# Low-rank up-projections of a recurrence, cut into eight pieces, each followed by a dense projection

## The chip, the core and the metric

The kernel runs on one core of a Trainium2 chip. A core has a matrix engine (TensorE, PE in the profile; its weight loads are PEld), a vector engine (DVE), a scalar engine (ACT), GpSimd (POOL) and a sync engine (SP), which here issues every DMA. Each engine works through its own list of instructions in order and waits at an instruction until the semaphores that it names have come. The metric is the device time of one execution in microseconds, the median over runs.

## What is computed

One layer of a model with 1024 tokens and 1024 channels: a norm, one wide projection, an attention branch with three kinds of keys, a recurrent branch (RWKV-7), a gated merge, and a feed-forward block with a short convolution. All inputs are float32. What matters for the change, shortened:

```
h = _rms_norm(x, norm_mix);  u = h @ w_in
q, kc, vc, ks, vs, kw, vw, nsa_gl, rw, merge = _split(u, IN_SPLITS)
o_nsa = _nsa(q, kc, vc, ks, vs, kw, vw, nsa_gl, ...)        # attention
# recurrent branch, on z = rw
z = z + mu * (z_prev - z)                                   # token shift
r, k, v, wd, ad, gd = _split(z, RWKV_SPLITS)                # 512,512,512,64,64,128 columns
w = -softplus(-(w0 + tanh(wd) @ w_up)) - 0.5;  decay = exp(-exp(w))
a = sigmoid(a0 + ad @ a_up)
g = sigmoid(gd) @ g_up
kh = k * (1 + (a - 1) * k_a);  kk = normalised k * k_k per head
y = _wkv7_scan(r, decay, kh, v, -kk, kk * a)                # then norm, bonus, * g
y = gates[0] * (o_nsa @ proj_nsa) + gates[1] * (o_rwkv @ proj_rwkv);  x = x + y @ w_out
x = x + _conv_ffn(_rms_norm(x, norm_ffn), ffn_up, ffn_conv, ffn_down)
```

The products with `w_up`, `a_up` and `g_up` (64, 64 and 128 rows) are the low-rank up-projections.

## The kernel before

Activations lie transposed, channels on partitions and tokens along the free axis, in two halves of 512 tokens. A dense projection (`project`, line 229) makes 128 output columns: `wload` (line 214) loads a weight tile `wraw` of 512 KB, ACT copies it to a rounded `whi`, POOL makes the rest `wlo`, and `mm3` (line 224) then does 24 matmuls of 128 x 512 for each half of the tokens into a PSUM tile `psP`. A whole projection is thus 48 matmuls at line 226. Tiles tagged "P" take turns on two PSUM banks, so a third one waits until the first has been read out.

The program is written as one chain of attention work (`attention`, a generator) into which a list of **fillers** is woven: the attention yields weights, and each time they sum to one, one filler is emitted behind it with a priority 10000 lower. A scheduler then sets the order on each engine by these priorities and a timeline of its own. So PE does attention where that scheduler expects it to be ready, and fillers elsewhere. After the attention, the remaining fillers are emitted in a row.

The fillers are:

- `zproj(g)`, line 575: one of 14 projections for the recurrence. Each half is shifted by one token with ACT (line 582) and DVE (line 583) into a tile `zs` and stored to `z_d`. `zs` is a ring of three buffers (`NZS`), which all fillers share. Projection 12 is [wd, ad], 13 is gd, 0 to 3 are r, 4 to 7 k, 8 to 11 v.
- `loraproj`, line 809, a generator: for each half `h` it loads `zwa` and `zg` (projections 12 and 13), takes tanh, and then for each of four column blocks `j` does three float32 matmuls (line 825): decay, `a` and gate. Each has its own `psP` tile. ACT takes tanh of the first two into a `zs` tile (line 831) and copies the third (line 828); POOL scales (lines 835 and 838); four tiles are stored by DMA to `lw_d`, `km_d`, `al_d` and `gt_d`. In the trace a float32 matmul stands as two records. Before the change the generator yields once for each half, after its four blocks.
- `prelude(j, h)`, line 745, in three steps, eight of them: it reads back r, k and the four low-rank results of one block and half and makes the operands of the recurrence. Its second step starts with a matmul at line 781, its third does 32 small ones at line 798. It stores to `ar_d`, `rk_d`, `bk_d` and `ad_d`.
- `mproj(m, halves)`, line 592: 16 projections for the gates, the last eight of them for one half only here (24 matmuls); the other halves follow later.

The attention goes through four pairs of heads. The projection of the next pair's queries (`qproj`, line 424) also uses "P" banks: its result stays in the bank until a norm (`rms64`: ACT line 297, PE line 299, ACT lines 301 and 302, DVE line 303) has read it.

Weight column groups of `w_t` are numbered: 4 to 7 are the queries, 8 to 21 are `zproj` 0 to 13, 22 to 37 are `mproj` 0 to 15.

When the attention and the listed fillers are done, the recurrence starts. Its first load (`gmk`, then `AD` for a small triangular solve) waits for the PE matmul with which the last projection of the first part ends, since its tiles take over the memory of that part.

## Time and profile before

| what | value |
|---|---|
| time, median of 3 runs | 1833.86 us (1833.84 to 1838.98) |
| span of the profiled execution, first to last instruction | 1828.3 us |
| granted TensorE clock, mean | 0.984 |
| DVE busy | 1168.6 us (64%) |
| ACT busy | 856.7 us (47%) |
| POOL busy | 773.4 us (42%) |
| first and last low-rank matmul start | 159.5 and 267.4 us |

The profiled execution's own time outside the span is not given; the median lies 5.6 us above its span. Busy time of PE includes the time in which matmuls run at a lower clock, and the ends of matmuls are modelled, so that a busy PE is not always one at full speed. In a timeline a row gives start, length, engine, line, operation, tiles, and in brackets the idle time ahead of it and what ended it. In a table of windows a row gives the stretch, its length, busy time (and number of instructions) of PE, PEld, DVE, ACT and POOL, the granted clock, the DMA share and GB/s.

### The profile page before, as it was taken

The numbers are of one execution on the slowest core, as the hardware profiler recorded it, in microseconds if no ns is written. First come the engines' busy times: TensorE is split into PE (matmuls) and PEld (weight loads), VectorE is DVE, ScalarE is ACT, GpSimd is POOL, SyncE is SP. The second block draws the span as 40 slices with busy tenths as digits, with TensorE's granted clock in tenths as the row PEclk, the third lists the DMA queues.
The fourth block names the chain that finished last, engine by engine and source line by source line (L and its number), as shares of the span: only waits on it lengthen the run. The fifth ranks groups of instructions, "written<-read, shape, count | busy, mean of one in ns | idle before, by whom it ended". The sixth has DMA issues, their size and how long they took to land.

```text
span 1828.3 us, 30848 instructions
## 1 busy us (share of the span) xinstructions
PE 1764.1 (96%) x11890; PEld 1375.4 (75%) x11890; DVE 1168.6 (64%) x2005; ACT 856.7 (47%) x1574; POOL 773.4 (42%) x500
## 2 busy tenths in 40 slices
PE   8999999999999999999999979998999999999998
PEld 5885657776777778777777768886888888888886
DVE  6214656777776511984445364419998899886798
ACT  5234665657656632455555454333443343534330
POOL 5212133131333325211234545566455444667757
PEclk9998999999999999899999989999999999999999
DMA  5415143231334435445553465343332222433302
GB/s 179 127 53 172 42 156 104 68 121 58 119 131 136 132 125 187 153 150 171 168 180 116 159 207 166 115 144 127 127 117 97 87 81 89 163 140 127 127 12 104
DMA packets 133443, 230.19 MB, mean 126 GB/s; under 512 B 25008, under 2 KB 54064, under 8 KB 133040
## 3 DMA queue, kind: packets, MB, share of 16 engines
q1 hardware_dynamic: 133296, 228.21, 37.6%
q8 instruction: 94, 1.54, 0.3%
q14 instruction: 53, 0.43, 0.1%
HBM read 159.39 MB, written 63.96 MB: 122 GB/s over the span
## 4 chain that ended last, share of the span: by engine, by line
PE 40%; DVE 7%; issue 1%; ACT 1%; DMA 1%; POOL 1%; POOLq 0%; DVEq 0%; SPq 0%; ACTq 0%
PE psP L226 9%; PE psM L1389 5%; PE psA L1389 3%; PE psP L1389 3%; PE psA L226 3%; PE psB L1499 2%; PE psA L1499 1%; PE psM L1499 1%; PE psP L1499 1%; PE psB L226 1%; PE psP L1570 1%; DVE u L1265 1%; PE psA L1570 1%; PE psM L1570 1%; PE psB L1570 1%
## 5 line engine op out<-in xcount | busy, mean ns | idle before, releaser
L220 POOL TENSOR_TENSOR wlo<-wraw,whi 128x1024 fp32r<-128x1024 f32 (+1 forms) x106 | 231.1, 2185 | 409.1 <-ACT whi L219 151.2
L226 PE MATMUL psP<-hhi,whi 128*128 128x512 f32 x784 | 319.3, 408 | 15.1 <-ACT hhi L706 8.9
L226 PE MATMUL psP<-hlo,whi 128*128 128x512 f32 x784 | 316.1, 404 | 3.8 <-DVE hlo L707 2.4
L226 PE MATMUL psP<-hhi,wlo 128*128 128x512 f32 x784 | 208.5, 399 | 0.0
L226 PEld LDWEIGHTS psP<-hhi,whi 128*128 128x128 f32 x784 | 149.3, 191 | 51.3 <-ACT hhi L706 10.6
L226 PEld LDWEIGHTS psP<-hlo,whi 128*128 128x128 f32 x784 | 149.3, 191 | 38.9 <-DVE hlo L707 3.8
L226 PEld LDWEIGHTS psP<-hhi,wlo 128*128 128x128 f32 x784 | 146.1, 190 | 31.8 <-issue 0.5
L219 ACT ACTIVATE whi<-wraw 128x1024 fp32r<-128x1024 f32 (+1 forms) x106 | 101.8, 961 | 131.6 <-PE psP L226 76.8
L543 DVE TENSOR_TENSOR pl<-pf,ph 128x512 f16<-128x512 f32 (+3 forms) x208 | 123.6, 604 | 44.2 <-ACT pf L542 43.2
L541 ACT ACTIVATE ph<-psA 128x512 f16<-128x512 f32 (+3 forms) x208 | 99.3, 477 | 62.1 <-PE psA L536 43.8
L484 DVE TENSOR_REDUCE mp<-psM 128x1 f32<-128x512 f32 (+1 forms) x192 | 94.5, 514 | 45.4 <-PE psM L482 38.5
L542 ACT ACTIVATE pf<-psA 128x512 f32<-128x512 f32 (+3 forms) x208 | 99.9, 480 | 0.0
L1330 POOL TENSOR_TENSOR wlo<-wraw,whi 128x1024 fp32r<-128x1024 f32 (+1 forms) x34 | 73.5, 2163 | 54.8 <-PE psM L1389 20.3
L546 PEld LDWEIGHTS <-ph 128*128 128x128 f16 x592 | 55.8, 97 | 22.6 <-issue 12.3
L565 POOL TENSOR_TENSOR onat<-onat,ot 128x256 f32<-128x256 f32 x32 | 25.0, 783 | 111.8 <-DVE ot L564 88.8
L551 PEld LDWEIGHTS <-pl 128*128 128x128 f16 x592 | 55.4, 99 | 20.7 <-DVE pl L543 6.5
L1329 ACT ACTIVATE whi<-wraw 128x1024 fp32r<-128x1024 f32 (+1 forms) x34 | 30.8, 910 | 64.1 <-issue 29.7
L549 PEld LDWEIGHTS <-ph 128*128 128x128 f16 x592 | 56.1, 98 | 2.1 <-issue 2.0
L1273 DVE SCALAR_TENSOR_TENSOR th<-th,u 128x512 f32<-128x512 f32 x34 | 56.8, 1670 | 0.4
L1330 POOL TENSOR_TENSOR s34l<-s,s34h 128x1024 fp32r<-128x1024 f32 x12 | 30.0, 2498 | 61.5 <-ACT s34h L1329 61.5
L721 DVE SCALAR_TENSOR_TENSOR fu<-psP,par,fu 128x511 f32<-128x511 f32 (+1 forms) x40 | 29.9, 746 | 34.9 <-ACT cvl L719 34.3
L969 DVE STREAM_TRANSPOSE AT<-AD 128x1024 f32<-128x1024 f32 x2 | 4.4, 2187 | 68.0 <-DMA sg_d<-zs 68.0
(711 smaller groups left out, 4879.0 us busy)
## 6 DMA issues: line engine op xcount, KB each, us to landing
wraw<-f_up SPq DMA_DIRECT2D x64, 512.0 KB, 3.3
wraw<-w_t SPq DMA_DIRECT2D x46, 512.0 KB, 3.8
wraw<-f_dn SPq DMA_DIRECT2D x22, 512.0 KB, 3.9
th_d<-th SPq DMA_DIRECT2D x34, 256.0 KB, 2.1
sg_d<-zs SPq DMA_DIRECT2D x32, 256.0 KB, 2.0
wraw<-w_out SPq DMA_DIRECT2D x16, 512.0 KB, 3.4
z_d<-zs SPq DMA_DIRECT2D x28, 256.0 KB, 2.4
x<-xT SPq DMA_DIRECT2D x24, 256.0 KB, 5.6
```

What stands on the lines that cost most here:

```text
L219: A.activation(hi[:, :nk], raw, AF.Copy)
L220: G.tensor_sub(lo[:, :nk], raw, hi[:, :nk].bitcast(F32))
L226: T.matmul(ps, a[:, k], ks_(b, k), start=(n == 0), stop=(n == 3 * nk - 1))
L484: V.reduce_max(mp[:, x, br, t:t + 1], pm[:, 0:(b1 - b0) * 128], axis=AX.X)
L541: A.activation(ph[0:nkey, rg], pa[0:nkey, rg], AF.Exp, scale=0.125)
L542: A.activation(pf[0:nkey, rg], pa[0:nkey, rg], AF.Exp, scale=0.125)
L543: V.tensor_sub(pl[0:nkey, rg], pf[0:nkey, rg], ph[0:nkey, rg])
L1273: V.scalar_tensor_tensor(th, th, 0.5, ub, op0=ALU.mult, op1=ALU.mult)
L1330: G.tensor_sub(lo[:, ks], raw[:, ks], hi[:, ks].bitcast(F32))
L1389: T.matmul(bank, w[wi][:, o_ + k], xs_[k][xi], start=start and n == 0, stop=n == 11, skip_group_check=True)
L1499: T.matmul(pj, x[:, m], y, start=(n == 0), stop=(n == 5))
L1570: T.matmul(pj, w[x][:, 4 * kp + j], hs[kp][y], start=(n == 0), stop=(n == 5))
```

## The change

`loraproj` now yields after each column block, so it comes in eight pieces of three matmuls, and each piece is put into one filler with a dense projection behind it. The order of the dense projections changes with it: before, 12, 13, 0, half of the low-rank work, 4, the other half, 8, then the preludes with the other nine between their steps; now 12, 13, 0, then a piece each with 4, 1, 5, 2, 6, 3, 7 and 8, then the preludes with 9, 10, 11 and the gate projections between their steps. Since a piece and a projection are one filler, more is emitted for the same number of filler turns.

```
-                yield
+                    yield
...
         lo_ = loraproj()
-        fillers = [(zproj, 12), (zproj, 13), (zproj, 0), (step, lo_), (zproj, 4), (step, lo_), (step, lo_), (zproj, 8)]
-        rest = [(zproj, q_ + j_) for j_ in range(1, 4) for q_ in (0, 4, 8)] + mp_
+        def lproj(gi):
+            step(lo_)
+            zproj(gi)
+
+        fillers = [(zproj, 12), (zproj, 13), (zproj, 0)] + [(lproj, g_) for g_ in (4, 1, 5, 2, 6, 3, 7)] + [
+            (lproj, 8), (step, lo_)]
+        rest = [(zproj, g_) for g_ in (9, 10, 11)] + mp_
         for j_ in range(4):
             for h_ in range(2):
                 g_ = prelude(j_, h_)
                 fillers += [(step, g_), rest.pop(0), (step, g_), rest.pop(0), (step, g_)]
```

The number of instructions and their operands stay the same; the order moves. Three places matter. Lines up to 840 keep their numbers.

On PE at the start of the low-rank work before (line 825 is low-rank, 478 and 482 are attention scores):

```order
L825 MATMUL psP<-zwa,lora 128x512
L825 MATMUL psP<-zg,lora 128x512
L478 LDWEIGHTS qd
L478 MATMUL psM<-k1s_322,qd 128x512
L478 LDWEIGHTS qd
L478 MATMUL psM<-k1s_322,qd 128x256
L482 LDWEIGHTS identb
L482 MATMUL psM<-cb,identb 128x128
L825 MATMUL psP<-zwa,lora 128x512
```

The same place on PE now, where the last rows are the dense projection 4 (line 226):

```order
L825 MATMUL psP<-zwa,lora 128x512
L825 MATMUL psP<-zg,lora 128x512
L478 LDWEIGHTS qd
L478 MATMUL psM<-k1s_322,qd 128x512
L478 LDWEIGHTS qd
L478 MATMUL psM<-k1s_322,qd 128x256
L482 LDWEIGHTS identb
L482 MATMUL psM<-cb,identb 128x128
L226 MATMUL psP<-hhi_107,whi 128x512
L226 MATMUL psP<-hlo_115,whi 128x512
```

After three low-rank matmuls, 48 dense ones stand where nine more low-rank matmuls stood; all eight pieces look like this.

On PE at the norm of the third pair's queries (line 299 is the norm's matmul, 532 to 536 and 551 are attention) before:

```order
L532 MATMUL psA<-qd,k1w_326 128x512
L534 LDWEIGHTS k2w_327
L534 MATMUL psA<-q_2965,k2w_327 128x512
L536 LDWEIGHTS identb
L536 MATMUL psA<-cb,identb 128x128
L299 MATMUL psM<-nsq,cst_f 128x512
L532 LDWEIGHTS k1w_326
```

The end of the same norm on PE now, its second half (the rows just ahead of these are the end of the query projection itself, line 226, with the norm's first half two matmuls before its end, and eight short matmuls of line 490):

```order
L490 LDWEIGHTS qd
L490 MATMUL psM<-k1c_332,qd 128x64
L492 LDWEIGHTS identb
L492 MATMUL psM<-cb,identb 128x512
L299 MATMUL psM<-nsq,cst_f 128x512
L226 MATMUL psP<-hhi_107,whi 128x512
L226 MATMUL psP<-hlo_115,whi 128x512
```

Before, attention matmuls stood between the query projection and both halves of its norm; now the norm follows at once, and the next dense projection (number 9) follows the norm.

On PE at the last prelude (line 798 is its third step, 226 the gate projections, 570 the last step of the attention) before:

```order
L226 MATMUL psP<-hhi_91,wlo 128x512
L570 MATMUL psA<-cst_f,onat 128x128 x8
L226 MATMUL psP<-hhi_92,wlo 128x512
L798 MATMUL psP<-lw,BK 64x64 x16
L226 MATMUL psP<-hhi_107,whi 128x512
```

And now (line 551 is attention):

```order
L551 LDWEIGHTS pl
L551 MATMUL psB<-Vc,pl 128x65
L226 MATMUL psP<-hhi_113,wlo 128x512
L226 MATMUL psP<-hhi_114,wlo 128x512
L798 MATMUL psP<-lw,BK 64x64 x16
L226 MATMUL psP<-hhi_107,whi 128x512
```

Before, 240 dense matmuls stood between this step and the start of the recurrence, and 48 between the prelude's second step and this one; now there are 72 and 24. From the start of the recurrence on, PE's order is as before up to the seam where the recurrence ends and the feed-forward block begins; there some matmuls of lines 226 change places with each other.

## The prediction

> **What bounds the kernel now.** I read the page first, then windows over the stretch that the change reorders, then the timeline of PE, ACT and SP there.
>
> ```profile
> span 1828.3 us, 30848 instructions
> PE   8999999999999999999999979998999999999998
> PEclk9998999999999999899999989999999999999999
> ```
>
> PE is busy nearly everywhere, so time can only be won where PE idles or runs at a lower clock. Both are seen in the fourth slice (137 to 183 us), where the low-rank matmuls begin.
>
> ```profile
> 716.74 1.99 PE L226 MATMUL psP<-hhi,wlo 128*128 128x512 f32 x8
> ...
> 718.76 0.33 SPq L139 DMA_DIRECT2D gmk<-cst  x1
> 719.14 0.43 SPq L139 DMA_DIRECT2D AD<-ad_d  x1
> ...
> 723.94 2.26 DVE L969 STREAM_TRANSPOSE AT<-AD 128x1024 f32<-128x1024 f32 x1 [67.97 <-DMA sg_d<-zs]
> ```
>
> These rows fix the far end. The recurrence starts when the last projection of the first part ends (718.7 us), although DVE has by then been idle for most of 68 us: the start is tied to PE's matmul, not to the preludes. PE does the same matmuls between 159.5 us and this point before and now. So the change is worth what idle time and slow clock it takes from or adds to these 559 us; the rest shifts with it.
>
> ```profile
> 159.50:184.90 25.40, 22.50 (x71) 7.88 (x70) 11.66 (x22) 7.99 (x13) 9.32 (x12) 0.80 0.52 175
> 196.60:224.90 28.30, 24.84 (x328) 16.72 (x327) 24.51 (x60) 23.49 (x55) 3.08 (x2) 1.00 0.06 20
> 239.00:267.80 28.80, 25.93 (x204) 12.71 (x204) 18.10 (x35) 17.91 (x39) 10.88 (x13) 0.94 0.46 160
> 316.40:339.20 22.80, 21.57 (x276) 14.15 (x276) 21.22 (x53) 18.08 (x46) 3.45 (x3) 1.00 0.07 25
> 339.20:413.10 73.90, 73.90 (x639) 54.35 (x637) 52.05 (x111) 43.67 (x102) 21.79 (x16) 1.00 0.37 113
> 443.00:663.50 220.50, 217.48 (x1847) 162.04 (x1845) 136.26 (x278) 127.44 (x294) 75.25 (x52) 1.00 0.38 125
> 663.50:718.60 55.10, 55.09 (x241) 45.22 (x242) 0.00 (x0) 16.58 (x23) 19.98 (x9) 1.00 0.42 139
> ```
>
> The columns after the length are busy time of PE, PEld, DVE, ACT and POOL. The first and third rows are the two low-rank halves: PE idles 2.90 and 2.87 us and the clock is 0.80 and 0.94. The second and fourth are attention without dense matmuls after a query projection (3.46 and 1.23 us idle). Where dense projections are mixed in (fifth and sixth rows) PE idles 3.02 us in 294, at full clock.
>
> **What the low-rank block costs.**
>
> ```profile
> 159.49 1.12 PE L825 MATMUL psP<-zwa,lora 64*128 64x512 f32 x2
> ...
> 168.24 1.12 PE L825 MATMUL psP<-zwa,lora 64*128 64x512 f32 x2 [1.45 <-ACT zs L828]
> ...
> 171.36 2.07 PE L825 MATMUL psP<-zwa,lora 64*128 64x512 f32 x2
> ...
> 243.49 1.12 PE L825 MATMUL psP<-zg,lora 128*128 128x512 f32 x2 [1.70 <-ACT zs L831]
> ...
> 167.59 0.60 ACT L828 ACTIVATE zs<-psP 128x512 f32<-128x512 f32 x1 [4.56 <-DMA lw_d<-zs]
> ```
>
> Each block of three matmuls fills four `zs` tiles, and the ring has three: the gate's copy (line 828) waits until the decay's store has landed, 4.56 us in this row. ACT stands still, the PSUM bank stays full, and PE waits for the bank (1.45 us). The next matmul then takes 2.07 us where the same took 1.12.
>
> ```profile
> 166.75:170.17 3.42, 1.97 (x7) 0.77 (x7) 1.14 (x3) 1.97 (x3) 0.62 (x1) 1.00 0.63 228
> 170.17:180.41 10.24, 10.24 (x22) 3.49 (x21) 3.54 (x7) 2.57 (x4) 3.38 (x5) 0.50 0.56 196
> 241.85:245.26 3.41, 1.77 (x4) 0.59 (x4) 2.37 (x3) 2.46 (x7) 3.33 (x3) 1.00 0.00 0
> 245.26:248.67 3.41, 3.41 (x17) 1.40 (x16) 2.32 (x6) 1.77 (x3) 1.36 (x2) 0.50 0.73 226
> 412.50:415.90 3.40, 2.18 (x25) 1.61 (x25) 0.77 (x3) 0.45 (x1) 3.15 (x4) 1.00 0.22 78
> ```
>
> Here the clock falls to 0.50 for 10.24 and 3.41 us, each time after 3.4 us in which PE was busy 58% and 52%. After a 64% busy one (last row) it stays at 1.00. So the gaps of 1.45 and 1.70 us seem to have cost the clock as well: half of 10.24 is 5.12 us, half of 3.41 is 1.71.
>
> The Trainium skill, "TensorE: Matmul & The Clock Gate", section "HAM oscillation — how this bites in real kernels", gives as the abstract rule "no PE-idle gaps >~3.4µs". By it gaps of 1.45 and 1.70 us would be harmless, the slow clock would have another cause, and the sum below would lose its clock term; these rows speak against that, since both slow stretches begin right behind the two longest gaps. It is the first rival below.
>
> **The sum, part by part**, against the span of 1828.3 us:
>
> 1. *Idle in the two low-rank halves*: between 0 and -5.77 us. Now 48 dense matmuls, about 12 us by 0.25 us each (eight in the 1.99 us of the row at 716.74), follow each three low-rank ones, so the gate's bank has longer than the 4.56 us wait before it is needed. Every piece takes its three ACT, three POOL and four DMA instructions along. On SP they now stand ahead of weight loads, each issue 0.3 to 0.4 us; a store that waits for ACT holds the weight load behind it, but the next weights are loaded a projection ahead, 12 us. I take -5.2: some tenths stay in eight pieces.
> 2. *Clock*: -6.83 us if no window falls under the 58% any more; 0 if it is not due to gaps. I take -6.8.
> 3. *Attention without dense matmuls*: three such stretches before (the third, 413.1 to 443.0, follows the same pattern), two now, 358 and 394 matmuls where before 324, 274 and 346 stood. The 1.23 us of the fourth row go: -1.2, between 0 and -2.4 if the two others shrink too.
> 4. *The third query projection*: its norm now has nothing but eight short matmuls beside it.
>
> ```profile
> 333.83 0.59 PE L299 MATMUL psM<-nsq,cst_f 128*128 128x512 f32 x1
> ...
> 334.68 0.71 ACT L301 ACTIVATE nrs<-psM,epst 128x512 f32<-128x512 f32 x1
> ...
> 335.99 0.68 ACT L302 ACTIVATE nrs<-nrs 128x512 f32<-128x512 f32 x1
> ...
> 337.04 0.68 ACT L297 ACTIVATE nsq<-psP 128x512 f32<-128x512 f32 x1
> ```
>
>    In PE's order the second half's matmul (line 299) waits for ACT's square, which in ACT's order stands behind 301 and 302 of the first half: 0.71 + 0.68 + 0.68 = 2.1 us plus hand-overs behind PE's first norm matmul, against some 1.2 us of PE work between (two dense matmuls, eight short ones, one of 512). An idle time of about 1.5 us is near the ones that cost a slow window. I take +1.9: 1.5 and a quarter of 1.71. Bounds: 0, and 1.5 + 5.12 = 6.6 with three slow windows, as the first gap had. Queued behind the waiting matmul are projection 9 and the attention of the third pair.
> 5. *The end of the preludes*: the second and third step of the last one now have one half projection between them.
>
> ```profile
> 646.21 1.02 PE L781 MATMUL psP<-t,cst_f 128*128 128x512 f32 x2
> ...
> 651.42 0.68 DVE L785 TENSOR_TENSOR kk<-kk,t 128x512 f32<-128x512 f32 x1
> ...
> 654.00 0.69 DVE L789 TENSOR_TENSOR BK<-al,cum 128x512 f32<-128x512 f32 x1 [1.18 <-POOL al L788]
> ```
>
>    From 646.21 to 654.69 the chain took 8.5 us, beside attention's work on DVE and ACT. The cover is 24 x 0.25 = 6.0 us and 40 attention matmuls, some 2 us. I take +1.0 for the last preludes together, between 0 and 2.5 each for three.
> 6. *The first prelude beside projection 8*: its ACT steps now stand ahead of that projection's read-out (+0.5, between 0 and 1), and the seam behind the recurrence: 0, with one slow window (1.71) either way.
>
> Sum: -5.2 - 6.8 - 1.2 + 1.9 + 1.0 + 0.5 = -9.8 us. The span becomes 1818.5 us. The runs' median stands 5.6 us above the profiled span, so the forecast is 1833.9 - 9.8 = **1824.1 us**.
>
> **Rivals.**
>
> - *The slow clock stays.* The low-rank matmuls with 64 of 128 rows, or a phase of the clock's own, slow PE, not the gaps. Then term 2 goes and the gain is 3.0: 1830.9 us. For it: the gap at 168 us is followed by three slow windows, though PE was busy in them. Against: the first low-rank row, before any gap, is at full speed (1.12 us).
> - *The wait moves to the query projection.* Term 4 at its upper bound, 6.6 instead of 1.9: the gain is 5.1, 1828.8 us. For it: the order of the rows; against: the scheduler put a first norm matmul two ahead of the projection's end.
> - *The end turns into waits; slower.* The tail of 55 us, pure dense work with PE idle 0.01 us, takes in the last three preludes with half projections between their steps. If attention has run out there, each of three preludes waits 8.5 - 6.0 = 2.5 us, which is more than the idle time ahead of both slow stretches and so brings a slow 10.24 us (5.1 us): 3 x 7.6 = 22.8 in place of 1.0, which turns the gain of 9.8 into a loss of 12.0 us: 1845.9 us. It decides from the point where fewer than about 7.5 us of attention work (3 x 2.5) are left for the three gaps. Against: attention stands among the rows up to the last third step, and DVE and ACT have room.
> - *It doesn't do what it says*: the order shows that it does.
> - *More is won*: term 3 at its end, terms 4 to 6 at 0: -14.4, 1819.5 us; 1815 us if a slow window at the seam (1.7) and most of the 3.0 us idle in the sixth row of the first windows go too.
>
> **How the numbers follow.** Chances: forecast 0.60, clock stays 0.12, query projection 0.14, end of the preludes 0.07, more 0.07. The range from 1815 to 1832 us takes in all but the third rival and some of the forecast's spread. A measurement of this kernel can tell about 0.3%, 5.5 us, from no change (1828.4 to 1839.4 us). Faster by more: 0.58 of the forecast, 0.07 of the wins, half of the query case (0.07): 0.72. Within: 0.20. Slower: 0.08.
>
> **What would show it.** Right: the gate's copy (line 828) without a wait that PE feels; the clock at 1.00 from 159 us to the start of the recurrence; that start at about 709 us; from there on the same distances as before. Term 4 shows as idle time ahead of line 299 or the dense matmul behind it, with the clock after it; term 5 as idle time ahead of line 798. Wrong: a new slow window in the stretch, DVE or ACT behind the attention in the preludes, or a recurrence that starts earlier and ends no sooner.

## The result and the profile after

| | before | after |
|---|---|---|
| time, median | 1833.84 us | 1846.31 us |
| ratio after / before | | 1.0083, 95% interval 1.0062 to 1.0105 |
| span of the profiled execution | 1828.3 us | 1845.8 us (its time 1847.62 us) |
| issue of `gmk`, the start of the recurrence | 718.76 us | 735.37 us (forecast: about 709) |
| from there to the end of the span | 1109.5 us | 1110.4 us |

The change made the kernel 12.5 us slower by the medians (0.8%) where the forecast had it 10 us faster. The two profiled executions differ by more, 17.5 us in span: the span of the kernel before lies 5.5 us under its median time, that of the changed kernel 0.5 us. So some 5 us of the differences read from the two profiles are spread between executions. In the profiles all but 1 us of the loss lies ahead of the recurrence, as the prediction said that any difference would. The page of the changed kernel (span, PE's busy time, granted clock in 40 slices):

```profile
span 1845.8 us, 30848 instructions
PE 1769.7 (96%) x11876; PEld 1375.4 (75%) x11890; DVE 1186.2 (64%) x2005; ACT 857.9 (46%) x1574; POOL 774.6 (42%) x500
PEclk9999999999999999989999989999999999999999
```

The dent of the clock in the fourth slice is gone, yet the span is longer. Where the time went is seen in windows of the changed kernel (busy PE, PEld, DVE, ACT, POOL; clock):

```profile
159.50:187.80 28.30, 28.18 (x123) 19.87 (x123) 10.34 (x17) 6.93 (x10) 6.77 (x5) 1.00 0.35 112
187.80:224.90 37.10, 29.86 (x359) 20.12 (x360) 28.64 (x72) 24.51 (x57) 3.57 (x3) 0.91 0.05 16
224.90:251.00 26.10, 23.29 (x147) 15.03 (x146) 12.85 (x33) 16.19 (x31) 5.07 (x7) 0.93 0.27 81
655.90:729.70 73.80, 64.10 (x519) 48.09 (x517) 41.76 (x62) 42.02 (x97) 32.09 (x21) 0.95 0.49 157
```

The first row is what was hoped for: the first piece and its projection, PE idle 0.12 us, full clock. The second is attention behind the second query projection (7.2 us idle), the third the second piece and its projection (2.8 us), the fourth the last preludes (9.7 us idle). In the kernel before, the stretch from the first low-rank half's end to the same norm had 3.5 us idle in 40, at full clock:

```profile
184.90:224.90 40.00, 36.54 (x389) 26.05 (x385) 25.95 (x65) 26.80 (x60) 4.22 (x5) 1.00 0.13 41
```

What PE waits for in the second and third window, in the timeline of the changed kernel:

```profile
189.03 0.38 PE L478 MATMUL psM<-k1w,qd 128*128 128x512 f16 x1 [0.67 <-DVE mp L484]
...
192.67 0.39 PE L490 MATMUL psM<-k1c,qd 128*128 128x64 f16 x8 [0.67 <-DVE mp L484]
194.95 1.03 PE L504 MATMUL psM<-identh,Mt 128*128 128x128 f16 x8 [1.89 <-DVE Mt L500]
...
231.51 0.75 DVE L303 SCALAR_TENSOR_TENSOR qn<-psP,par,nrs 128x512 f32<-128x512 f32 x1 [1.94 <-ACT nrs L302]
232.32 1.12 PE L825 MATMUL psP<-zwa,lora 64*128 64x512 f32 x2 [2.12 <-DVE qn L303]
```

Scores (lines 478 to 490) that used to stand between low-rank matmuls now stand alone, and PE waits for DVE's maxima (0.67 us, four times) and for the matrix made of them (1.89 us). The second piece waits 2.12 us for a "P" bank that the query norm still reads. In the last window DVE is late, and with it the preludes:

```profile
688.11 4.53 DVE L543 TENSOR_TENSOR pl<-pf,ph 128x128 f16<-128x128 f32 x4
...
688.39 2.37 POOL L220 TENSOR_TENSOR wlo<-wraw,whi 128x1024 fp32r<-128x1024 f32 x1
...
691.10 0.20 PE L551 MATMUL psB<-Vw,pl 128*128 128x65 f16 x1 [2.22 <-DVE pl L543]
...
711.56 2.34 POOL L220 TENSOR_TENSOR wlo<-wraw,whi 128x1024 fp32r<-128x1024 f32 x1
711.63 2.81 DVE L789 TENSOR_TENSOR BK<-al,cum 128x512 f32<-128x512 f32 x1 [1.17 <-POOL al L788]
...
714.50 0.98 PE L798 MATMUL psP<-lw,BK 64*64 64x64 f32 x32 [3.26 <-DVE BK L789]
```

PE stands 3.26 us ahead of a prelude's third step (line 798), which waits for a DVE operation of 2.81 us; in the prediction's rows that operation took 0.69. The gap of 2.22 us is not a prelude's: it stands ahead of an attention matmul (line 551), which waits for four small DVE operations of the attention (4.53 us together) that ran partly beside a POOL subtraction.

The whole stretch up to the recurrence, split in both kernels where the first of the eight half projections begins (before, then after):

```profile
159.50:674.84 515.34, 499.31 (x4269) 352.54 (x4268) 328.44 (x715) 305.38 (x685) 150.10 (x124) 0.99 0.34 111
674.84:718.76 43.92, 43.92 (x193) 36.06 (x192) 0.00 (x0) 13.23 (x16) 19.30 (x8) 1.00 0.42 144
```

```profile
159.50:656.26 496.76, 477.80 (x3911) 336.44 (x3924) 304.34 (x654) 276.50 (x603) 136.95 (x111) 0.99 0.32 103
656.26:735.37 79.11, 69.41 (x536) 52.45 (x536) 41.40 (x61) 43.32 (x98) 34.14 (x22) 0.96 0.49 155
```

Up to that point PE idles 16.0 us before and 19.0 after; from there on 0 and 9.7.

The clock follows such gaps here too. These are the 3.41 us ahead of each of the four stretches in which the changed kernel's clock falls to 0.50 before the recurrence (for 6.8, 3.4, 3.4 and 3.4 us):

```profile
190.16:193.57 3.41, 1.48 (x16) 0.90 (x16) 2.26 (x7) 0.00 (x0) 0.28 (x1) 1.00 0.43 153
231.06:234.47 3.41, 1.97 (x7) 0.81 (x8) 2.03 (x5) 2.89 (x6) 1.31 (x2) 1.00 0.12 26
688.44:691.85 3.41, 1.18 (x24) 0.80 (x21) 3.41 (x3) 3.38 (x9) 3.18 (x2) 1.00 0.86 277
712.36:715.77 3.41, 0.98 (x32) 0.84 (x32) 3.30 (x7) 0.53 (x2) 1.98 (x2) 1.00 0.11 38
```

PE was busy 29 to 58% in each, as in the two cases of the prediction.

### The profile page after: what moved, and what is told of

Same layout as the page of the kernel before. It is cut to its first block, busy times and chain, and to the rows that moved or that the text cites. A ratio compares the mean times of both kernels' runs of the same rounds, so it can differ in the third digit from the quotient of the medians.

```text
span 1845.8 us, 30848 instructions
## 1 busy us (share of the span) xinstructions
PE 1769.7 (96%) x11876; PEld 1375.4 (75%) x11890; DVE 1186.2 (64%) x2005; ACT 857.9 (46%) x1574; POOL 774.6 (42%) x500
## 4 chain that ended last, share of the span: by engine, by line
PE 40%; DVE 7%; issue 1%; DMA 1%; POOL 1%; ACT 1%; SPq 0%; POOLq 0%; DVEq 0%; ACTq 0%
PE psP L226 9%; PE psM L1394 5%; PE psA L1394 3%; PE psP L1394 3%; PE psA L226 3%; PE psB L1504 2%; PE psA L1504 1%; PE psM L1504 1%; PE psP L1504 1%; PE psB L226 1%; PE psP L1575 1%; DVE u L1270 1%; PE psB L1575 1%; PE psM L1575 1%; PE psA L1575 1%
## 5 line engine op out<-in xcount | busy, mean ns | idle before, releaser
L226 PE MATMUL psP<-hhi,wlo 128*128 128x512 f32 x784 | 212.6, 401 | 0.0
L543 DVE TENSOR_TENSOR pl<-pf,ph 128x512 f16<-128x512 f32 (+3 forms) x208 | 133.8, 653 | 67.3 <-ACT pf L542 60.9
L565 POOL TENSOR_TENSOR onat<-onat,ot 128x256 f32<-128x256 f32 x32 | 28.8, 904 | 84.3 <-DVE ot L564 82.4
L1335 POOL TENSOR_TENSOR s12l<-s,s12h 128x1024 fp32r<-128x1024 f32 x12 | 31.4, 2620 | 34.4 <-PE psA L1394 21.3
```

What stands on the lines that cost most here:

```text
L226: T.matmul(ps, a[:, k], ks_(b, k), start=(n == 0), stop=(n == 3 * nk - 1))
L543: V.tensor_sub(pl[0:nkey, rg], pf[0:nkey, rg], ph[0:nkey, rg])
L1335: G.tensor_sub(lo[:, ks], raw[:, ks], hi[:, ks].bitcast(F32))
```

## The experiments

The loss has three suspects: the **cut** into pieces, the **order** of the dense projections that comes with it, and what either does to covers. In each run the start of the recurrence (issue of `gmk`, in one profiled execution) shows the part in question; the ratio is that of many executions to the kernel before in the same session. Executions of one kernel spread by some 5 us to either side, so a start alone is good to a few microseconds; where it and the median disagree, the median counts. Where an expectation speaks of excess over bare matmul time, every matmul of the program is counted at the pace of an undisturbed row (0.21 us for 512 columns, in proportion for fewer, 0.86 for 512 float32 columns), and the sum is taken from PE's time. Traces lack a few matmul records, so such figures are rough, and the readings below go by idle time and clock. Edits shift line numbers by up to thirteen.

| run | edit | start, us | median, us | ratio to before (95%) |
|---|---|---|---|---|
| e1 | change, first low-rank half uncut | 726.78 | 1843.6 | 1.0063 (1.0043 to 1.0083) |
| e2 | change, whole projections last | 737.31 | 1863.2 | 1.0167 (1.0137 to 1.0196) |
| e3 | e1 and e2 | 731.47 | 1875.4 | 1.0234 (1.0207 to 1.0261) |
| e4 | before, four more tiles | 719.47 | 1832.3 | 0.9991 (0.9976 to 1.0007) |
| e5 | before's blocks, change's order | 734.16 | 1845.5 | 1.0066 (1.0046 to 1.0086) |
| e6 | half uncut, half with half projections | 720.93 | 1835.1 | 1.0020 (1.0004 to 1.0036) |
| e7 | pieces with half projections | 728.39 | 1844.5 | 1.0061 (1.0039 to 1.0084) |
| e8 | before, five more tiles | 729.32 | 1846.2 | 1.0068 (1.0048 to 1.0087) |
| e9 | change, half projections in pairs | 726.18 | 1838.6 | 1.0030 (1.0020 to 1.0041) |
| e10 | e9 and e1 | 724.85 | 1841.0 | 1.0051 (1.0025 to 1.0078) |
| e11 | e8, table load mended | 717.83 | 1833.2 | 0.9995 (0.9982 to 1.0008) |
| e12 | change, half projections' `wlo` on DVE | 729.19 | 1841.9 | 1.0045 (1.0026 to 1.0064) |
| e13 | before, all `wlo` on DVE | 725.57 | 1839.0 | 1.0018 (1.0000 to 1.0037) |
| e14 | e9, all `wlo` on DVE | 724.70 | 1839.3 | 1.0020 (1.0000 to 1.0039) |
| e15 | before, rate of fillers 1.4 | 709.01 | 1827.0 | 0.9963 (0.9948 to 0.9978) |
| e16 | e11 with that rate | 716.47 | 1830.4 | 0.9988 (0.9971 to 1.0004) |

### e1: the first half in one block again

```
-fillers = [z12, z13, z0] + [(lproj, g_) for g_ in (4, 1, 5, 2, 6, 3, 7)] + [(lproj, 8), (step, lo_)]
+fillers = [z12, z13, z0, (lblock,), z4] + [(lproj, g_) for g_ in (1, 5, 2, 6)] + [z3, z7, z8, (step, lo_)]
```

(`lblock` does four steps; z12 stands for `(zproj, 12)`.)

> The changed kernel, but the first four low-rank pieces stand in a row again, ahead of dense projection 4 (the other four stay cut up). Theory (uncovered waits): in the changed kernel the attention scores behind the first query projection lost the low-rank matmuls that stood among them (the stretch 187.8 to 224.9 us has 13.6 us over its bare matmul time, 6.4 before), and the second piece waits 2.1 us for a PSUM bank that the norm holds, with slow clock behind. With the block back, both should go (about -7 and -5 us), the first low-rank half should cost its wait on the zs ring and slow clock again (about +8), and the tail ahead of the recurrence should keep its waits. The recurrence, which starts at 735.2 us in the changed kernel and 718.6 before, should start at 729 to 733 us, and the time be 1840 to 1844 us. Rival (each piece costs by itself, about 2 us for its queues, whatever stands around it): the scores keep their waits and half of the 16.6 us goes: start at 727 us, without any change of idle time behind the first query projection.

Windows of e1, the block and then the stretch to the same norm:

```profile
159.30:181.40 22.10, 19.31 (x71) 6.91 (x70) 11.65 (x22) 7.97 (x12) 9.36 (x12) 0.92 0.57 195
181.40:218.30 36.90, 34.34 (x372) 24.84 (x368) 23.98 (x60) 23.74 (x52) 4.23 (x5) 1.00 0.15 48
```

The block waits again (2.8 us, with a clock of 0.92), and the scores behind it are back at 2.6 us idle and full clock; the wait for the bank is gone. The block holds 20 score matmuls (line 478) again, as in the kernel before; the changed kernel's first window holds 12. The start came 8.6 us earlier, but this was the fastest of e1's nine executions; the medians differ by 2.7 us, and the intervals overlap, so the times do not show a gain. The tail kept most of its loss. The windows show that the low-rank block and the scores covered each other.

### e2 and e3: whole projections last

```
-rest = [(zproj, g_) for g_ in (9, 10, 11)] + mp_
+rest = [(zproj, g_) for g_ in (9, 10, 11)] + mp_[NMF:] + mp_[:NMF]
```

> The changed kernel, but the order of the 16 mixing projections is turned round: the eight half ones (24 matmuls) come first, and whole ones (48 matmuls, about 12 us) stand between the steps of the last preludes. Theory (half projections are too short a cover for a prelude's step): the gaps of 2.2 and 3.3 us and both slow windows of 3.4 us in 656 to 730 us go, which is 9 to 11 us: the recurrence starts at 724 to 727 us and the time is 1835 to 1838 us. The half ones stand beside attention then and may add 0 to 3 us there. Rival (the last preludes are late because DVE and ACT have a backlog, which no order of PE's work mends): gaps of over 2 us stay ahead of line 798, and less than 4 us is won.

> Both edits together: first four pieces in a row, and whole projections between the last preludes' steps. Theory: the two places are apart from each other, so the gains add: recurrence at 718 to 723 us, time 1829 to 1834 us, no slower than the kernel before. Rival (pieces cost by themselves, or the loss only moves): it stays over 1838 us, and new gaps stand at another place of the stretch from 160 to 735 us.

Both missed. The scheduler also set another order inside the recurrence in these two, which then took 1119 and 1140 us in place of 1110, so only the part ahead of it is read. Windows of e2, first the preludes with half projections, now in the middle of attention, then those with whole ones at the end:

```profile
505.20:606.40 101.20, 92.35 (x772) 65.89 (x769) 78.99 (x139) 60.69 (x142) 49.28 (x32) 0.93 0.53 167
606.40:726.60 120.20, 119.11 (x1003) 88.91 (x1000) 62.11 (x124) 66.34 (x155) 39.72 (x27) 1.00 0.37 118
```

The tail is clean as the theory had it (1.1 us idle in 120), but the loss moved along with the half projections: 8.9 us idle in 101, although attention stood beside them. That they could hide there was the part of the expectation that fell. So the end of attention is not what costs. The longest gaps there (1.83, 1.72 and 1.50 us) stand ahead of attention matmuls that wait for DVE, and none over 0.4 us ahead of a prelude's step: with half the dense work between two steps, attention itself goes uncovered.

### e4, e8 and e11: is the waiting in the low-rank halves worth anything?

e4 takes the gate's tile out of the `zs` ring of the kernel before; e8 takes decay and gate out, into five tiles in turn; e11 is e8 with the load of the combined table behind the last decay too:

```
 # e4
+if q == 2:
+    t = prep.tile([128, 512], F32, name="gtm", tag=("kk", "t1", "cum", "e2")[j], bufs=1)
 # e8
+if q != 1:
+    t = prep.tile([128, 512], F32, name="gtm", tag=("kk", "t1", "cum", "e2", "km")[(8 * h + 2 * j + q // 2) % 5], bufs=1)
 # e11, besides
-with tc.issue_after(last.ins):
+with tc.issue_after(last.ins), tc.issue_after(lastd.ins):
```

> The kernel before, with one edit: the low-rank gate's tile lies in four tiles of the preludes that are free at that time, not in the zs ring of three, so that nothing in a block waits for a store to land. Theory (terms 1 and 2 of the prediction: idle time and slow clock in the two halves are from that ring): idle time of 5.8 us falls under 1.5, the slow windows of 10.2 and 3.4 us go, and the recurrence starts 10 to 12.5 us earlier, at 706 to 709 us; time 1822 to 1825 us. Rival (the slow clock is not due to these gaps): the idle time goes but the slow windows stay, 4 to 5 us won, 1829 us. Second rival (with the ring free, ACT becomes the limit of the block: four read-outs of about 0.6 us per three matmuls of 1.1 us): 2 to 4 us of idle time stay.

In e4 the wait moved one instruction on. In its timeline, the issue of the first decay's store and the second block's decay, which now waits for it:

```profile
164.09 0.44 SPq L842 DMA_DIRECT2D lw_d<-zs  x1
...
168.79 0.69 ACT L834 ACTIVATE zs<-psP,pd 128x512 f32<-128x512 f32 x1 [3.69 <-DMA lw_d<-zs]
```

The store let the tile go 4.7 us after its issue. So the prediction's reading (four tiles in a ring of three) was too narrow: this store took longer to land than the first block lasted (4.2 us, from 160.6 to 164.8 us). The waits were still there, so e4, level with the kernel before, does not say what they are worth.

> The kernel before, with decay and gate of the low-rank work in five free tiles of the preludes in turn, so that a tile comes back after two and a half blocks of three matmuls and the zs ring of three holds two tiles of a block. With four extra tiles the wait only moved from the gate's copy to the next decay (a store takes 4.7 us to land, a block of three matmuls with its scores 3 to 4 us). Theory (terms 1 and 2 of the prediction, idle time and slow clock are due to waits for landing stores): idle time ahead of the low-rank matmuls under 1 us, no slow window in 160 to 270 us, start at 706 to 711 us, time 1821 to 1826 us. Rival (the scores' reductions on DVE and ACT's read-outs limit the block as soon as the stores don't): idle time of over 3 us stays in the halves, ahead of the scores (line 478) or in the stretches behind them, and start is at 714 us or later.

e8 removed the waits but came out 13 us slower, for a reason outside both theories. ACT in its timeline, and its table loads by line:

```profile
257.33 1.28 ACT L846 ACT_TABLE_LOAD   x1
...
260.50 1.28 ACT L835 ACT_TABLE_LOAD   x1
261.79 0.69 ACT L835 ACTIVATE gtm<-psP,pd 128x512 f32<-128x512 f32 x1
```

```profile
L783 ACT ACT_TABLE_LOAD x8 | 10.3, 1283 | 0.1
...
L541 ACT ACT_TABLE_LOAD x7 | 9.0, 1283 | 0.1
```

One tanh of a decay came behind the load of the combined exp and log table and threw it out; from there on preludes and attention loaded tables in turn, 54 loads in the run where the kernel before has 28.

> The kernel before with decay and gate in five free tiles, as in the run that came out slower, but the load of the combined exp and log table waits for the last decay too, so that no tanh comes behind it. Theory: that run lost about 10 us because ACT loaded tables 54 times instead of 28 (the tanh behind the preload threw the combined table out); with 28 loads its front is left, where the low-rank halves lose 12 us of waits and slow clock but the scores behind them lose cover: start at 713 to 716 us, time 1827 to 1831 us. Rival (the attention's own chain over DVE and ACT sets the length of the stretch up to the first norm, whatever the low-rank matmuls wait for): start at 717 to 720 us, no change that can be measured.

With 28 loads again, e11 is the clean test. Its windows (low-rank half, then the stretch to the second pair's query norm), its longest wait in the second, and the second half of that norm in e11 and in the kernel before:

```profile
159.10:174.10 15.00, 14.87 (x46) 5.21 (x46) 7.82 (x14) 7.87 (x12) 9.01 (x11) 1.00 0.72 252
174.10:219.10 45.00, 39.76 (x408) 27.41 (x406) 28.79 (x72) 26.62 (x59) 4.96 (x5) 0.96 0.13 46
```

```profile
189.97 0.65 PE L504 MATMUL psM<-identh,Mt 128*128 128x128 f16 x8 [1.67 <-DVE Mt L500]
```

```profile
223.80 1.02 PE L299 MATMUL psM<-nsq,cst_f 128*128 128x512 f32 x2
```

```profile
224.43 1.02 PE L299 MATMUL psM<-nsq,cst_f 128*128 128x512 f32 x2
```

The half takes 15.0 us in place of 25.4, with PE idle 0.13 us at full clock: the waits of terms 1 and 2 are gone from their place. But it holds 13 score matmuls where the kernel before had 20, so less work stands in it. The rest stands bare in the stretch behind, which takes 45.0 us in place of 40.0; at the norm's second half 0.6 us of the gain is left, and 0.9 at the start of the recurrence. From 159.5 us to that start PE idles 18.1 us in place of 16.0, and half clock costs 3.4 in place of 6.8 (half of its length). The ratio of the times is 0.9995 (0.9982 to 1.0008). The rival stands: the waits of the low-rank halves were not worth removing.

### e5: the order alone

```
 # blocks uncut, yield as before the change
+fillers = [z12, z13, z0, (step, lo_), z4, z1, z5, z2, (step, lo_), z6, z3, z7, z8, (step, lo_)]
```

> The dense projections in the changed kernel's order, so that eight of them are used up ahead of the preludes and five half ones stand between the last preludes' steps, but the low-rank work uncut, in its two blocks of four. Theory (what costs in the tail is that whole projections were used up early and half ones, some 6 us, cover a step of 8.5 us): the tail from the sixth whole mixing projection on loses 10 to 14 us though nothing is cut up, and the two blocks keep their waits: the recurrence starts at 727 to 733 us (718.6 before, 735.2 in the changed kernel). Rival (the pieces themselves, with their stores and queues, delay the preludes behind them): start at 718 to 722 us with a clean tail.

The start moved to 734.16 us, by 15.4 of the change's 16.6 us, with nothing cut. This was the slowest of e5's six executions, but the medians say the same: 12.3 us over the kernel before, where the change lies 12.5 over it. The tail in e5, from the second half projection on, and its longest wait ahead of a third step:

```profile
671.90:728.50 56.60, 48.87 (x325) 37.06 (x324) 24.05 (x39) 27.93 (x59) 26.69 (x16) 0.93 0.53 165
```

```profile
693.15 0.68 PE L798 MATMUL psP<-lw,BK 64*64 64x64 f32 x16 [2.87 <-DVE BK L789]
```

7.7 us idle and a clock of 0.93. The longest gap of all, 3.28 us, stands ahead of the attention's last step (line 570), which waits for POOL. The rival (the pieces delay the preludes) fell. This run also moves the question: the change's cost is the order of the dense projections; in that order the cut itself comes out near zero.

### e6 and e7: half projections behind the pieces, whole ones in the preludes

```
 # e6
+fillers = [z12, z13, z0, (lblock,), z4] + [(lproj, m_) for m_ in (8, 9, 10, 11)] + [(step, lo_), z8]
 # e7
+fillers = [z12, z13, z0] + [(lproj, m_) for m_ in (8, 9, 10, 11)] + [z4] + [(lproj, m_) for m_ in (12, 13)] + [(step, lo_), z8, (step, lo_), (step, lo_)]
 # both: lproj(m_) does mproj m_ (one half) behind the piece, and the preludes have their order of before
```

> First four low-rank pieces in a row, the other four each followed by a half mixing projection (24 matmuls), and the preludes with the whole projections between their steps, as before the change. Theory (uncovered waits in two places, each mended by itself): the first experiment lost about 10 us in the tail, which go; its front stays: excess over bare matmul time of 60 to 63 us where the kernel before had 63, start at 714 to 719 us, time 1826 to 1832 us. Rival (6 us of dense work behind a piece is too little for its stores of 4.7 us, so that a wait for the ring comes back): idle time ahead of the low-rank matmuls of over 2 us in all, start at 720 us or later.

> All eight low-rank pieces cut up as in the change, six of them each followed by a half mixing projection, and whole projections between the preludes' steps. Theory: the loss of the tail (12 to 16 us) goes, the uncovered scores behind the first query projection and the bank wait at the second piece stay (about 7 and 5 us): start at 718 to 723 us, time 1830 to 1836 us. Rival (the cut itself costs, or the last preludes are late because attention has run out by then): gaps of over 2 us ahead of the last preludes' third steps, start over 727 us.

In both the tail is clean: from 640 us on PE idles 1.2 us in all in e6 and 2.7 in e7. The starts and times missed. e6 kept two waits of 1.4 and 1.7 us ahead of low-rank matmuls, one in each half, and ended 2 us behind the kernel before. e7, 11 us behind it, kept the uncovered scores and the wait for the bank, and its third query norm came ahead of the load of the combined table, which cost four more table loads (32) and gaps up to 2.5 us at 340 to 360 us. Moving whole projections back to the preludes mends the tail; the front is another matter, and in e7 the pieces do cost there.

### e9 and e10: half projections in pairs

```
-rest = [(zproj, g_) for g_ in (9, 10, 11)] + mp_
+rest = [(zproj, g_) for g_ in (8, 9, 10, 11)] + mp_[:NMF] + [(pair, 8, 9), (pair, 10, 11), (pair, 12, 13)] + mp_[14:]
 # the eighth piece has no projection behind it; e10 has the first block uncut besides, as e1
```

> The changed kernel with all its pieces cut, but projection 8 goes into the first prelude instead of behind the eighth piece, and six of the half mixing projections stand in pairs (48 matmuls, as much as a whole one) between the last preludes' steps; only the very last gap has a single half one. Theory (the loss of the tail is the missing cover of half projections): the stretch from the sixth whole mixing projection to the recurrence, 16.7 us over bare matmul time in the changed kernel (62 to 80), falls to 6 to 9 us, the front stays as it is (38 to 39 us over bare time up to the first prelude's second step), the recurrence starts at 723 to 728 us and the time is 1834 to 1839 us. Rival (the last preludes are late because attention is used up or DVE and ACT have a backlog): start at 731 us or later, with gaps of over 2 us ahead of lines 781 or 798.

> The same, and the first four low-rank pieces in a row as before the change. Theory (two separate losses, both mended): the front gains about 6 us more, as the first experiment's did (excess of 32 us in place of 39 where the first prelude begins): start at 716 to 721 us, time 1827 to 1832 us, level with the kernel before or a little faster. Rival (the gains don't add): start at 724 us or later.

The tail of e9:

```profile
649.30:720.40 71.10, 68.89 (x529) 52.75 (x527) 35.59 (x59) 40.86 (x91) 36.32 (x23) 1.00 0.55 175
```

2.2 us idle at full clock, in place of 9.7 at 0.95; start and time came as expected, with an interval clear of the change's, and the pieces are all still there. This shows what the tail's loss hangs on: how much dense work stands between the preludes' steps. With the tail clean e9 is still 5.8 us over the kernel before, so the front of the changed order costs as well. e10 missed: its front was 6.9 us ahead at the first prelude's second step (391.6 us in place of 398.5; half of that is a shorter slow stretch), but by the start 1.3 us of it were left, and the medians don't show a gain. From that step on PE idles 12.5 us in place of 9.3, and a slow stretch costs 1.7 us more.

### e12, e13 and e14: does POOL's subtraction stretch DVE?

```
-G.tensor_sub(lo[:, :nk], raw, hi[:, :nk].bitcast(F32))
+(V if lov[0] else G).tensor_sub(lo[:, :nk], raw, hi[:, :nk].bitcast(F32))
 # lov[0]: in e12 for the eight half projections, in e13 (on before) and e14 (on e9) from the attention's start to the recurrence
```

> The changed kernel, but the low part of the eight half projections' weights (the subtraction of line 220, 2.3 to 2.4 us on POOL) is computed on DVE, so that POOL has no long two-operand work while the last preludes run. Theory (half projections are too short a cover): a prelude's step still takes 7 to 8 us, the gaps ahead of lines 781 and 798 shrink but stay, 0 to 4 us are won, start at 731 to 736 us. Rival (DVE's stretched operations, 2.8 us in place of 0.7 while POOL works, are what makes the preludes late): no DVE operation of a prelude takes over 1.5 us there, the gaps over 2 us go, and start is at 725 to 729 us.

> The kernel before, with the weights' low parts (line 220) computed on DVE (1.2 us each) instead of POOL (2.35 us) from the attention's start to the recurrence. Theory (POOL's subtraction only costs where a prelude is late already; where attention stands bare no weights are prepared): start at 716 to 720 us, time within 0.3% of the kernel before. Rival (it stretches DVE's operations all through attention, and that delays PE): start at 710 to 715 us, time 1824 to 1829 us.

> The changed kernel with half projections in pairs, and the low parts on DVE in the same stretch. Theory (the pairs have removed the whole loss of the tail, so nothing is left for this to win there): start at 723 to 727 us (726.0 with the pairs alone). Rival (the two mends add, 6 us more): 718 to 721 us.

The tail of e12, the subtraction on DVE, and the operation that took 2.81 us in the changed kernel (shortest, median, longest in ns):

```profile
656.60:723.50 66.90, 62.45 (x531) 47.07 (x528) 40.89 (x71) 43.42 (x99) 19.19 (x14) 0.97 0.53 170
```

```profile
685.84 1.21 DVE L220 TENSOR_TENSOR wlo<-wraw,whi 128x1024 fp32r<-128x1024 f32 x1
```

```profile
L793 DVE TENSOR_TENSOR BK<-al,cum x8: 677/692/693, 419.9 to 705.9; 128x512 f32<-128x512 f32 x8
```

4.5 us idle in place of 9.7; the largest gap is 2.0 us, ahead of a dense matmul that waits for ACT, and none over 0.3 us is left ahead of lines 781 and 798. The start came 6.2 us earlier (4.4 by the medians): the rival's number, nearly. In the trace, then, both are at work, the short cover and the stretched DVE; the times alone don't show it, since e12's interval touches the change's. e14 shows that the two mends don't add: with pairs the tail is clean already. e13 gained nothing; its first low-rank half drew a long slow clock (28.4 us at 0.68), so its start says little.

```profile
160.00:188.40 28.40, 25.53 (x62) 8.58 (x61) 12.06 (x23) 8.19 (x13) 7.38 (x11) 0.68 0.43 157
```

### e15 and e16: the same dense work spread over more of attention

```
-RATE1 = 1.0
+RATE1 = 1.4
```

> The kernel before, with 1.4 filler turns for each that attention's work gave: the projections come earlier and stand closer in attention, which so reaches on into the half projections at the end (in the kernel before the last 55 us ahead of the recurrence were dense work alone). Theory (attention's chain over DVE and ACT sets the length of what stands without dense matmuls, so that the excess of PE is cut by spreading the same dense work over more of attention): 5 to 10 us less, start at 708 to 714 us, time 1823 to 1829 us. Rival (the stretches behind each query projection stay bare, since no turn falls into them, and only the order changes): start at 716 to 722 us. Against both: slow clock or a late prelude at the end, over 722 us.

> The same rate of 1.4, and decay and gate in five free tiles so that no low-rank matmul waits for a store. Theory (with a dense projection ahead of the scores the low-rank halves' waits are no longer cover, so that term 1 and 2 of the prediction come out now): 3 to 8 us less than the run with the rate alone. Rival (the stretch up to the first norms is attention's own length still): within 2 us of it.

e15 is faster than both kernels. PE's line of its page, its start, and two of its windows (low-rank half; attention behind it):

```profile
PE 1760.2 (97%) x11879; PEld 1373.9 (75%) x11890; DVE 1174.2 (64%) x2005; ACT 851.5 (47%) x1570; POOL 776.5 (43%) x500
```

```profile
709.01 0.33 SPq L139 DMA_DIRECT2D gmk<-cst  x1
```

```profile
159.70:181.80 22.10, 19.24 (x69) 7.11 (x70) 11.66 (x22) 7.98 (x12) 9.32 (x12) 0.92 0.58 194
181.80:238.80 57.00, 56.47 (x433) 36.40 (x431) 34.71 (x71) 36.56 (x77) 21.30 (x23) 1.00 0.44 152
```

The low-rank half waits as ever; but a dense projection and the second half stand among the scores now, and PE idles 0.5 us in 57, where the kernel before idled 3.5 in 40. Two things besides are different in e15. Its profiled execution drew one slow stretch of 3.4 us ahead of the recurrence, where the kernel before drew 10.2 and 3.4; that is 5.1 of the 9.8 us in the start, and the medians differ by 5.6. And it loads 24 tables in place of 28, since the second pair's query norm no longer stands between the tanh operations of the two low-rank halves. e16 loads 24 as well and is level with the kernel before, so the loads alone don't make the gain.

e16 takes the waits out of the halves and is 3.4 us slower than e15, which neither of its two expectations had: the halves are then over before the scores need them. Its stretch behind them:

```profile
204.20:244.10 39.90, 32.68 (x324) 22.66 (x322) 28.24 (x57) 21.94 (x52) 10.57 (x8) 0.96 0.30 91
```

7.2 us idle: the same as in the changed kernel.

## Why the prediction was wrong

- **The frame held.** The difference lies between 159.5 us and the start of the recurrence, and behind it 0.9 us were added (term 6's seam: 0). Split where the half projections begin, PE's idle time and what half clock costs together are 22.9 us before and 24.1 after up to there, and 0 and 13.1 from there to the start. So the front, forecast at -10.8 (terms 1 to 4 and 6), came out at +1.2, and the tail, forecast at +1.0, at +13.1; the other 2.3 of the 16.6 us are in PE's busy time. Both kernels do the same work in all, but not the same on each side of the split.
- **Terms 1 and 2 (-5.2 and -6.8) failed as gains.** The waits for the ring and the slow clock behind them went. The step that failed is the one before them, that idle time ahead of the low-rank matmuls is worth its length. e11 took it away alone and gained nothing; in the change the scores (3.8 us more idle, clock 0.91) and the wait for the bank (2.1 us and 3.4 us of half clock) took it back. While the low-rank matmuls waited for stores, the scores went on beside them: 20 score matmuls stood in the first half before, 13 in e11's half and 12 in the changed kernel's first window, and PE waited for the rest later. Term 2 also took the slow clock of one execution for that of all; behind the same block it lasted between 3.4 and 20.5 us from run to run.
- **Term 3 (-1.2) had the wrong sign**, from the same step: the first stretch of attention without dense matmuls idled 7.2 us in place of 3.5, since more of the scores now stood in it.
- **Term 4 (+1.9) was about right**: gaps of 0.3 to 0.8 us around the third query norm, no slow clock.
- **Term 5 (+1.0, bound 2.5 for each of three) is the term that cost the forecast its sign.** The largest gaps had about the foreseen size (2.2 and 3.3 us, each with 3.4 us of half clock), but all were taken at less than half of one gap on the ground that attention's matmuls fill them. The step that failed is this overlap: attention's own DVE work was late in the same places, and the gap of 2.2 us stands ahead of its matmuls, not of a prelude's. In all the tail lost 13.1 us, 9.7 idle and 3.4 by the clock. e5 puts the change's loss on the order of the projections, e9 on the half ones between two steps. The chain of 8.5 us was read from an undisturbed prelude; beside POOL's subtraction it grows, which e12 puts at some 4 to 6 us of the whole, with an interval that also allows little.
- **The third rival came true** in its mechanism, through the last two preludes and the attention beside them rather than three preludes. That its time (1845.9 us) was met is chance: it had 22.8 us lost in the tail and the front's gain kept, where 13.1 were lost and no gain was left.
- **The clock** followed the gaps. The Trainium skill, "TensorE: Matmul & The Clock Gate", section "HAM oscillation — how this bites in real kernels", gives 3.4 us without work as the limit. The four windows above, with gaps of 0.67 to 3.26 us, each led to half clock, so the traces still speak against it. But a gap doesn't always cost clock: in e1 PE waited 1.69 us at the second low-rank half, as long as the 1.70 us that the prediction priced, and the clock stayed at 1.00 behind this window with PE 50% busy:

```profile
237.70:241.10 3.40, 1.71 (x22) 0.80 (x18) 1.70 (x2) 2.67 (x7) 3.40 (x3) 1.00 0.00 0
```

Open: why the front's gain in e10 is given back later, how much of e12's gain is luck of the clock, and what in e15's new order makes its gain, as the rate moves everything at once. That attention's chain over DVE and ACT sets the length of its bare stretches is supported by e11, e15 and e16, but no run has changed that chain itself.

## What to carry over

Idle time of one engine is only worth removing where what the others do in the meantime isn't needed next: ask of each gap what it covers. Where pieces of work serve as cover, count them: using a whole projection at one place takes it from another, and a cover must be as long as the chain it hides under the load that runs beside it. The one order that came out faster here spread the same dense work over more of the attention. And an execution's slow stretches are partly luck, so a term for the clock needs more than one execution.

## What the hardware showed

A DVE operation on two tiles can be held up by POOL. The eight operations at line 789, before and after (shortest, median, longest in ns):

```profile
L789 DVE TENSOR_TENSOR BK<-al,cum x8: 691/692/693, 307.6 to 654.0; 128x512 f32<-128x512 f32 x8
```

```profile
L789 DVE TENSOR_TENSOR BK<-al,cum x8: 678/692/2810, 418.2 to 711.6; 128x512 f32<-128x512 f32 x8
```

The one of 2.81 us began 0.07 us behind a POOL subtraction and ended 0.54 us after it. Over all 18 traces, 54 operations of this size at lines 543, 785 and 789 began inside such a subtraction with at least 0.7 us of it to go; they took 1.34 to 2.91 us (median 2.38), while the median of the other 1818 was 0.69 and their longest 1.79. The Trainium skill, "SBUF — State Buffer", section "Who interferes with whom", says that a DVE instruction with two inputs in SBUF contends with a POOL instruction that reads SBUF, over ports that the two share under an exclusive lock. The rows agree. The same subtraction took 1.21 us on DVE and 2.34 to 2.37 on POOL.

Half clock ahead of the recurrence came in multiples of 3.41 us, and how many it was varied: at the first long wait of the uncut low-rank block (1.1 to 1.5 us) it lasted 3.4 us in e1 and e15, 6.8 in e6, 10.2 in the kernel before, 13.7 in e5 and 20.5 in e13.
